# Block-diagonal gate products of an RG-LRU with hi and lo parts stacked along the contraction

## The chip, the cores and the metric

The kernel runs on one core of a Trainium2 chip. The metric is the device time of one execution in microseconds; several runs are made and their median counts.

## The reference, cut to what matters

Two layers (DEPTH = 2) act on x of 256 tokens by 1024 features, all in float32. A layer is a feed-forward half step, a mixing block with two branches, a second feed-forward half step and a gate on a per-layer input. The change lies in the first branch of the mixing block, a gated linear recurrence over time (RG-LRU):

```python
def rg_lru(x, w_a, b_a, w_x, b_x, lam):          # 16 blocks of 64 x 64
    xb = x.reshape(B, S, RNN_BLOCKS, RNN_BW)
    r = jax.nn.sigmoid(jnp.einsum('bsnc,ncd->bsnd', xb, w_a).reshape(B, S, C) + b_a)
    i = jax.nn.sigmoid(jnp.einsum('bsnc,ncd->bsnd', xb, w_x).reshape(B, S, C) + b_x)
    log_a = -RG_C * r * jax.nn.softplus(-lam)
    a = jnp.exp(log_a)
    mult = jnp.sqrt(-jnp.expm1(2.0 * log_a))
    u = mult * (i * x)
    # h[t] = a[t] * h[t-1] + u[t]

for i in range(DEPTH):
    x = x + 0.5 * swiglu_ffn(...)
    rx, rgate, q, k, v, f_logit, ga, gb = split(rms_norm(x) @ w_in[i])
    ya = (rg_lru(causal_dwconv(rx)) * gelu(rgate)) @ w_rnn_out[i]
    yb = forgetting_attention(q, k, v, f_logit) @ w_attn_out[i]
    x = x + (sigmoid(ga) * ya + sigmoid(gb) * yb) @ w_o[i]
    x = x + 0.5 * swiglu_ffn(...)
    x = x + sigmoid(rms_norm(x) @ w_pg + b_pg) * (p[i] @ w_pe)
```

## The kernel before

Features lie on the 128 partitions, in KT = 8 tiles `m` of 128, and the S = 256 tokens lie along a row. Every product keeps float32 accuracy by splitting each operand into a part `hi`, rounded to the matmul type float32r, and the rest `lo`; TensorE (PE) then adds three products, hi by hi, hi by lo and lo by hi (`mm3`, L297 to L300, and `mm3m`, L302 to L305), or a variant with one 512-column and one 256-column matmul (`mm2`, L338 to L341), whose two halves `total` (L375 on ACT, L376 on DVE) adds.

Weights come from memory in 1 MB loads on SyncE's queue. Each load is cut into units of 128x1024. For each unit ScalarE (ACT) writes the hi part `wh` (L96) and VectorE (DVE) subtracts to get the lo part `wl` (L97). There are five buffers for `wh` and five for `wl`, so a new unit can be split only when PE is done with the unit five before.

The code states an order, with small steps that are put off (`defer`) and called one or two at a time between units (`tick`). The framework then orders the instructions of each engine anew, by a model of its own of how long each takes. Each engine runs its list strictly in that order: an instruction that waits holds up all that stand behind it.

In the mixing block `mix` of each layer the work runs like this:

- For each tile m the recurrence's input is projected, convolved on DVE into `xc` (L512) and split into `xch` (ACT, L516) and `xcl` (DVE, L517).
- The values v (four weight units) are computed. Between them and in the first q group, `gates(m)` (from L542) makes the two gate products of tile m. The weights of two 64x64 blocks stand in a 128x128 matrix whose other two quarters are zero. Three matmuls of 256 columns make the first gate, r, and three more the second, i. ACT applies a tanh to each (`thr` L548, `thi` L549). The step `s1` bounds thr (DVE, L553) and forms the decay `a` and its companions on ACT; `s2` forms `tq` and multiplies i into `xc` on DVE.
- When all eight tiles are there, `root` takes one square root over all of `tq` on ACT (L564, with a load of its function table ahead of it). `scan(m)` multiplies (L569) and runs the recurrence (L570) on DVE.
- Products for q and k (`qk`), their squared sums (ACT `qsq` L647, DVE L649) and their norms, whose power runs on GpSimd (POOL, L652), are followed by attention for eight heads. `step_a` transposes (`tr`, L685) and splits q and k (`aq` L692 and `ak` L693 are their lo parts). `step_b` makes the scores `s` (L704) and the probabilities `pr`. `step_c` transposes those (`pt`, L729) and ACT copies them to `ph` (L731). `step_d` makes the head's output `o<-ph,vh` (L739).
- Between these steps PE is given "filler" products `f` (L298 to L300) for the gates of the branches. Then follow `ya` (W_rnn_out), `yb` (W_attn_out) and, on four PSUM banks in turn, the output product `o<-mg` (L338 to L341).

Two pools matter. Tiles of 128x512 (`work2`, tag `w2`) have three buffers. PSUM has four banks called mm and four called at.

## Time and profile before

| | |
|---|---|
| median of 3 runs | 1318.01 us (1317.98 to 1318.56) |
| the profiled execution, whole | 1318.03 us |
| its span from first to last instruction | 1316.3 us (1.7 us lie around it) |
| PE busy | 1306.8 us, 99% of the span |
| DVE busy | 1069.5 us, 81% |
| ACT busy | 813.5 us, 62% |
| POOL busy | 34.8 us, 3% |
| granted PE clock | full in every slice |

The profile is one execution of the kernel. A row of a timeline gives the start in us, the duration in us, the engine, the source line and operation, the tiles written and read, and in brackets the idle time ahead of it with the instruction that ended it. Matmuls overlap: each lasts longer than the distance to the next one, so what one costs is the distance between starts.

### The profile page before, as it was taken

Reading aid. Unit: us, or ns where it says so; the run is one execution under the profiler, and the core shown is the slowest. Engines: PE = TensorE matmul, PEld = TensorE weight load, DVE = VectorE, ACT = ScalarE, POOL = GpSimd, SP = SyncE. Lnnn points to the kernel's source line nnn. Section 1 sums busy time; section 2 is a strip of 40 time slices with the busy share of each in tenths; the row PEclk is TensorE's granted clock in tenths of the full one; section 3 lists DMA queues with packets and bytes.
Section 4 is the critical chain, followed back from the end, with each engine's and each line's share of the span. In section 5 each row is a group of like instructions: output and inputs, shape, how many; then the busy total and the mean of one; then the engine's idle time right before and its main releaser. Section 6 shows DMA issues by size and latency. Waiting matters only on the chain.

```text
span 1316.3 us, 21929 instructions
## 1 busy us (share of the span) xinstructions
PE 1306.8 (99%) x8376; PEld 1188.0 (90%) x8376; DVE 1069.5 (81%) x2100; ACT 813.5 (62%) x1479; POOL 34.8 (3%) x44
## 2 busy tenths in 40 slices
PE   9999999999999999999999999999999999999997
PEld 8888899889999888889988888998899898888896
DVE  7998769899676899876789887697996678998765
ACT  6665657867664666565556556578676555665653
POOL 1000000020000000000000000000200000000000
PEclk9999999999999999999999999999999999999999
DMA  8654664445444555456545546654443445554660
GB/s 294 240 184 155 218 226 165 178 167 176 158 161 161 197 188 192 163 180 234 177 177 192 192 134 228 220 188 160 171 180 138 161 170 206 186 183 154 220 226 32
DMA packets 37256, 241.22 MB, mean 183 GB/s; under 512 B 4128, under 2 KB 4256, under 8 KB 14368
## 3 DMA queue, kind: packets, MB, share of 16 engines
q1 hardware_dynamic: 36864, 239.30, 51.6%
q8 instruction: 66, 1.08, 0.3%
q10 hardware_dynamic: 288, 0.52, 0.1%
q14 instruction: 38, 0.31, 0.1%
HBM read 238.76 MB, written 1.05 MB: 182 GB/s over the span
## 4 chain that ended last, share of the span: by engine, by line
PE 99%; DMA 0%; ACT 0%; DVE 0%; POOLq 0%; DVEq 0%; issue 0%
PE mm L341 20%; PE mm L339 11%; PE at L341 11%; PE at L339 6%; PE f L298 3%; PE f L300 3%; PE f L299 3%; PE qk L303 2%; PE qk L305 2%; PE qk L304 2%; PE mm L300 2%; PE mm L298 2%; PE mm L299 2%; PE mm L338 2%; PE ya L341 2%; PE at L338 2%
## 5 line engine op out<-in xcount | busy, mean ns | idle before, releaser
L97 DVE TENSOR_TENSOR wl<-wr,wh 128x1024 fp32r<-128x1024 f32 (+2 forms) x476 | 538.3, 1133 | 143.6 <-ACT wh L96 137.6
L96 ACT ACTIVATE wh<-wr 128x1024 fp32r<-128x1024 f32 (+2 forms) x476 | 467.3, 986 | 298.8 <-PE mm L341 91.3
L341 PE MATMUL mm<-h,wh 128*128 128x512 f32 x616 | 219.1, 394 | 0.0
L341 PE MATMUL at<-h,wh 128*128 128x512 f32 x616 | 218.6, 394 | 0.0
L339 PE MATMUL mm<-h,wl 128*128 128x256 f32 x704 | 182.3, 280 | 0.0
L339 PE MATMUL at<-h,wl 128*128 128x256 f32 x704 | 181.7, 281 | 0.0
L341 PE MATMUL mm<-f,wh 128*128 128x512 f32 x504 | 176.9, 394 | 0.0
L339 PE MATMUL mm<-f,wl 128*128 128x256 f32 x528 | 144.1, 280 | 0.0
L339 PEld LDWEIGHTS at<-h,wl 128*128 128x128 f32 x704 | 132.0, 188 | 8.8 <-ACT h L331 0.7
L339 PEld LDWEIGHTS mm<-h,wl 128*128 128x128 f32 x704 | 131.8, 188 | 7.8 <-DVE wl L97 0.4
L341 PEld LDWEIGHTS mm<-h,wh 128*128 128x128 f32 x616 | 115.6, 188 | 22.6
L341 PEld LDWEIGHTS at<-h,wh 128*128 128x128 f32 x616 | 114.9, 188 | 21.9
L341 PEld LDWEIGHTS mm<-f,wh 128*128 128x128 f32 x504 | 94.4, 188 | 20.8
L300 PE MATMUL f<-h,wl 128*128 128x256 f32 x384 | 108.5, 283 | 0.0
L298 PE MATMUL f<-h,wh 128*128 128x256 f32 x384 | 108.5, 283 | 0.0
L299 PE MATMUL f<-h,wh 128*128 128x256 f32 x384 | 108.1, 282 | 0.0
L339 PEld LDWEIGHTS mm<-f,wl 128*128 128x128 f32 x528 | 99.4, 188 | 2.1
L299 PEld LDWEIGHTS f<-h,wh 128*128 128x128 f32 x384 | 72.4, 188 | 0.1
L298 PEld LDWEIGHTS f<-h,wh 128*128 128x128 f32 x384 | 72.3, 188 | 0.1
L300 PEld LDWEIGHTS f<-h,wl 128*128 128x128 f32 x384 | 72.4, 188 | 0.0
L375 ACT ACTIVATE sum<-mm 128x256 f32<-128x256 f32 x112 | 40.1, 375 | 50.6 <-PE mm L341 50.4
L376 DVE TENSOR_TENSOR sum<-mm,sum 128x256 f32<-128x256 f32 x112 | 45.0, 419 | 14.8 <-ACT sum L375 14.8
(297 smaller groups left out, 2746.9 us busy)
## 6 DMA issues: line engine op xcount, KB each, us to landing
wr<-in_w2i SPq DMA_DIRECT2D x44, 1024.0 KB, 4.8
wr<-in_w1i SPq DMA_DIRECT2D x41, 1024.0 KB, 4.8
wr<-in_wf SPq DMA_DIRECT2D x32, 1024.0 KB, 4.8
wr<-in_w1o SPq DMA_DIRECT2D x32, 704.0 KB, 4.0
wr<-in_w2o SPq DMA_DIRECT2D x32, 704.0 KB, 4.1
wr<-in_wqk SPq DMA_DIRECT2D x16, 1024.0 KB, 4.8
wr<-in_wv SPq DMA_DIRECT2D x8, 1032.0 KB, 4.8
wr<-in_wro SPq DMA_DIRECT2D x8, 1024.0 KB, 4.8
```

Of the source, the lines that this page charges most:

```text
L96: self.nc.scalar.activation(out=hi[:, c], in_=src[:, c], func=AF.Copy)
L97: self.nc.vector.tensor_tensor(out=lo[:, c], in0=src[:, c], in1=hi[:, c].bitcast(F32), op=ALU.subtract)
L298: T.matmul(ps, lhsT=wh, rhs=xh, start=first, stop=False)
L299: T.matmul(ps, lhsT=wh, rhs=xl, start=False, stop=False)
L300: T.matmul(ps, lhsT=wl, rhs=xh, start=False, stop=last)
L303: T.matmul(ps, lhsT=xh, rhs=wh, start=first, stop=False)
L304: T.matmul(ps, lhsT=xh, rhs=wl, start=False, stop=False)
L338: T.matmul(ps, lhsT=wh, rhs=t, start=True, stop=False, skip_group_check=True)
L339: T.matmul(ps[:, 0:S], lhsT=wl, rhs=t[:, 0:S], start=False, stop=False, skip_group_check=True)
L341: T.matmul(ps, lhsT=wh, rhs=t, start=False, stop=last, skip_group_check=True)
L375: A.activation(out=o, in_=ps[:, S:], func=AF.Copy)
L376: V.tensor_tensor(out=o, in0=ps[:, 0:S], in1=o, op=ALU.add)
```

## The change

In `mix`, tiles are now handled in pairs. After the split of an odd tile m, three transfers on GpSimd's queue rearrange `xch` and `xcl` of tiles m-1 and m: the upper 64 rows of `xch` go to a scratch tile `sw`, the lower 64 rows of `xcl` go to the upper rows of `xch`, and `sw` goes to the lower rows of `xcl`. From then on `xch` holds hi and lo of the lower block, and `xcl` those of the upper block. Each transfer moves 64x512 numbers, 128 KB, and there are 12 of them in a layer.

The weights are laid out to match: each 64x64 block stands twice, once against hi and once against lo. Both gates of a block fill the 128 columns, the two in swapped order for the upper block. Two matmuls (hi and lo part of the weights) now make both gates of one block, four per tile in place of six. Of each block's 128 output rows, 64 belong to r and 64 to i. The tanh of each half goes to a 128x512 tile `tg`; two transfers of 64x256 numbers (64 KB) per tile, on GpSimd's queue, bring the i rows to their place in `thi`, and the bounding of thr is done in two operations of 64 partitions each. In a layer that makes 16 such transfers, so 28 transfers in all and 56 in two layers.

Last, the multiply of `scan` is marked to stay in program order.

```diff
@@ split of the recurrence's input
                 A.activation(out=xch[:, m], in_=xc[:, m], func=AF.Copy)
                 V.tensor_tensor(out=xcl[:, m], in0=xc[:, m], in1=xch[:, m].bitcast(F32), op=ALU.subtract)
+                if m % 2:
+                    c = slice(m - 1, m + 1)
+                    t = work2(F32R, "sw")[lower].rearrange("p (m s) -> p m s", m=2)
+                    G.dma_start(out=t, in_=xch[upper, c])
+                    G.dma_start(out=xch[upper, c], in_=xcl[lower, c])
+                    G.dma_start(out=xcl[lower, c], in_=t)
             defer(conv, split)
@@ gates(m)
-            for g in range(2):
-                c = slice((m * 2 + g) * P, (m * 2 + g + 1) * P)
-                mm3(ps[:, g * S:(g + 1) * S], wg_hi[:, c], wg_lo[:, c], xch[:, m], xcl[:, m], True, True)
+            for b, xs in enumerate((xch, xcl)):
+                c = slice((m * 2 + b) * P, (m * 2 + b + 1) * P)
+                T.matmul(ps[:, b * S:(b + 1) * S], lhsT=wg_hi[:, c], rhs=xs[:, m], start=True, stop=False)
+                T.matmul(ps[:, b * S:(b + 1) * S], lhsT=wg_lo[:, c], rhs=xs[:, m], start=False, stop=True)
             thr, thi, th, a2 = work(s="thr"), work(s="thi"), work(s="th"), work(s="a2")
-            A.activation(out=thr, in_=ps[:, 0:S], func=AF.Tanh, scale=0.5, bias=hcol(l, "ba", m))
-            A.activation(out=thi, in_=ps[:, S:], func=AF.Tanh, scale=0.5, bias=hcol(l, "bx", m))
+            t2 = work2(s="tg")
+            for b, own, other in ((0, lower, upper), (1, upper, lower)):
+                c = slice(b * S, (b + 1) * S)
+                A.activation(out=t2[:, c], in_=ps[:, c], func=AF.Tanh, scale=0.5, bias=hcol(l, ("ba", "bx")[b], m))
+                G.dma_start(out=thi[own], in_=t2[other, c])
             def s1():
-                V.tensor_scalar(out=thr, in0=thr, scalar1=-1.0, scalar2=None, op0=ALU.max)
+                for b, own in ((0, lower), (1, upper)):
+                    V.tensor_scalar(out=thr[own], in0=t2[own, b * S:(b + 1) * S], scalar1=-1.0, scalar2=None,
+                                    op0=ALU.max)
@@ scan(m)
-            V.tensor_tensor(out=tq[:, m], in0=tq[:, m], in1=xc[:, m], op=ALU.mult)
+            tc.keep_in_program_order(V.tensor_tensor(out=tq[:, m], in0=tq[:, m], in1=xc[:, m], op=ALU.mult))
```

The framework's order changes with it, on every engine. Lines 564, 569, 704, 729 and 739 of the kernel before are lines 580, 585, 720, 745 and 755 of the changed one.

On ACT, around the square root of layer 0, the kernel before had this order (a number behind a name tells tiles of one name apart; `wh_3097` and `wh_3117` of before are the same two units as `wh_3129` and `wh_3149` of the changed kernel):

```order
L96 ACTIVATE wh_3031<-wr_3029 128x1024
L622 ACTIVATE dh_3021<-dc_3016 128x256
L555 ACTIVATE th_2886<-thr_2884,sp 128x256
L556 ACTIVATE a_2887<-a_2506 128x256
L96 ACTIVATE wh_3053<-wr_3029 128x1024
L564 ACT_TABLE_LOAD
L564 ACTIVATE tq_2507<-tq_2507,tiny 128x2048
L647 ACTIVATE qsq_3069<-qk_2976 128x512
L96 ACTIVATE wh_3097<-wr_3095 128x1024
L96 ACTIVATE wh_3117<-wr_3095 128x1024
```

The changed kernel has this one:

```order
L96 ACTIVATE wh_3129<-wr_3127 128x1024
L570 ACTIVATE a_2518<-thr_2953,sp 128x256
L571 ACTIVATE th_2955<-thr_2953,sp 128x256
L663 ACTIVATE qsq_3110<-qk_3007 128x512
L572 ACTIVATE a_2956<-a_2518 128x256
L96 ACTIVATE wh_3149<-wr_3127 128x1024
L580 ACT_TABLE_LOAD
L580 ACTIVATE tq_2519<-tq_2519,tiny 128x2048
L96 ACTIVATE wh_3171<-wr_3169 128x1024
```

The table load and the square root have moved two weight units later. On PE, between the last transpose `tr` of the first head and that head's first score product, there stood 37 matmuls (8 `qk` of 512 columns and 29 `f` of 256); now 24 `f` stand there. Counted from the program's start, that score product has 21 matmuls of 256 columns less ahead of it: 16 of the gates and 5 `f`. On DVE, between the square root and the lo part `ak` of that head, there now stand 6 multiplies, 6 scans, 4 reduces, 4 products `qk`, 8 operations of four columns, 7 units `wl` and the lo part `aq`.

On PE, at the last head's probabilities, where the `ya` products end and the `yb` products begin, the changed kernel of layer 0 has:

```order
L339 MATMUL ya_4738<-yr_3674,wl_4636 128x256
L341 MATMUL ya_4738<-yr_3674,wh_4635 128x512
L745 MATMUL pt_4308<-ident,pr_4261 128x128 x3
L755 MATMUL o_4348<-ph_4312,vh_2520 128x256
L338 MATMUL yb_4763<-ot_3375,wh_4662 128x512
```

The head's output now stands right behind its transposes. Before, 26 matmuls of `ya` stood between the last of them and the output product. On ACT, ahead of the copy to `ph` that this product reads, the changed kernel has the total of the last `ya` bank and one weight unit:

```order
L738 ACTIVATE pr_4261<-pr_4261,rs_4263 128x128
L738 ACTIVATE pr_4261<-pr_4261,rs_4263 128x256
L375 ACTIVATE sum_4759<-ya_4738 128x256
L96 ACTIVATE wh_4766<-wr_4764 128x1024
L747 ACTIVATE ph_4312<-pt_4308 128x384
```

These stood in the same order in the kernel before, so what moved is PE's work between the transposes and their user.

On PE in the output product, between the last matmul of the first bank, `o_5036`, and the first of the fifth, `o_5159`, which takes over that bank, the changed kernel has 11 matmuls (7 of 512 columns, 4 of 256):

```order
L341 MATMUL o_5036<-mg_4928,wh_4897 128x512
L341 MATMUL o_5037<-mg_4928,wh_4932 128x512
L341 MATMUL o_5097<-mg_4928,wh_4968 128x512
L339 MATMUL o_5097<-mg_4928,wl_4969 128x256
L341 MATMUL o_5097<-mg_4928,wh_4968 128x512
L341 MATMUL o_5129<-mg_4928,wh_5002 128x512
L339 MATMUL o_5129<-mg_4928,wl_5003 128x256
```

Before, 21 stood there, among them all of the fourth bank, which the changed kernel begins ahead of the first bank's last matmul. ACT's and DVE's order is the same as before there: a weight unit, then the totals of the first two banks.

On GpSimd, layer 0 has this queue, whose transfers are sent in order:

```order
L524 DMA sw_2358<-xch_2195 64x512
L525 DMA xch_2195<-xcl_2196 64x512
L524 DMA sw_2436<-xch_2195 64x512
L526 DMA xcl_2196<-sw_2358 64x512
L525 DMA xch_2195<-xcl_2196 64x512
L524 DMA sw_2514<-xch_2195 64x512
L526 DMA xcl_2196<-sw_2436 64x512
L525 DMA xch_2195<-xcl_2196 64x512
L526 DMA xcl_2196<-sw_2514 64x512
L524 DMA sw_2581<-xch_2195 64x512
L563 DMA thi_2613<-tg_2616 64x256 x2
```

Before, GpSimd had no transfers, and in this stretch nothing but the eight powers of the q and k norms, which now stand behind the last `thi` transfer.

## Rows read from the trace of the kernel before

**Rows 1.** The page, busy time: engine, us busy (share of span), instructions.

```profile
PE 1306.8 (99%) x8376; PEld 1188.0 (90%) x8376; DVE 1069.5 (81%) x2100; ACT 813.5 (62%) x1479; POOL 34.8 (3%) x44
```

**Rows 2.** All waits of PE: line, releaser, us in total, times, longest.

```profile
PE warm L865 <- POOL ones L193: 1.1, 1, 1.1
PE at L338 <- ACT wh L96: 0.3, 1, 0.3
```

**Rows 3.** Window of layer 0: busy us of PE, PEld, DVE, ACT, POOL; PE clock.

```profile
200.00:302.00 102.00, 102.00 (x633) 93.41 (x632) 91.59 (x195) 73.80 (x125) 11.25 (x8) 1.00 0.50 179
```

**Rows 4.** Timeline of PE: first and twelfth matmul of the first gate pair.

```profile
222.76 0.28 PE L298 MATMUL g<-xch,wbh 128*128 128x256 f32 x1
...
224.06 0.28 PE L300 MATMUL g<-xch,wbl 128*128 128x256 f32 x1
```

**Rows 5.** Timeline of ACT around the square root of layer 0.

```profile
263.72 1.06 ACT L96 ACTIVATE wh<-wr 128x1024 fp32r<-128x1024 f32 x1 [0.32 <-PE qk L305]
264.80 1.28 ACT L564 ACT_TABLE_LOAD   x1
266.09 2.01 ACT L564 ACTIVATE tq<-tq,tiny 128x2048 f32<-128x2048 f32 x1
...
274.90 1.06 ACT L96 ACTIVATE wh<-wr 128x1024 fp32r<-128x1024 f32 x1 [1.75 <-PE qk L305]
```

**Rows 6.** Timeline of DVE from the square root to the first head's q and k.

```profile
268.13 2.44 DVE L569 TENSOR_TENSOR tq<-tq,xc 128x256 f32<-128x256 f32 x7 [2.09 <-ACT tq L564]
...
271.08 3.01 DVE L570 TENSOR_TENSOR_SCAN xc<-a,tq 128x256 f32<-128x256 f32 x5
...
287.39 0.22 DVE L650 TENSOR_SCALAR s<-s,s 128x4 f32<-128x4 f32 x1
287.52 0.69 DVE L655 TENSOR_TENSOR qk<-qk,s 128x512 f32<-128x512 f32 x1
288.13 1.22 DVE L97 TENSOR_TENSOR wl<-wr,wh 128x1024 fp32r<-128x1024 f32 x1
...
291.46 0.47 DVE L693 SCALAR_TENSOR_TENSOR ak<-tr,gqk,ak 128x256 fp32r<-128x256 f32 x1
```

**Rows 7.** Timeline of PE: last transpose of the first head, and its first score.

```profile
287.02 0.27 PE L685 MATMUL tr<-ident,qk 128*128 128x128 f32 x1
...
292.42 0.70 PE L704 MATMUL s<-ak,aq 128*128 128x256 f32 x5
```

**Rows 8.** Timeline of PE: the last head's transposes and the product that uses them.

```profile
390.60 0.38 PE L729 MATMUL pt<-ident,pr 128*128 128x128 f32 x2
...
395.35 0.28 PE L739 MATMUL o<-ph,vh 128*128 128x256 f32 x1
```

**Rows 9.** Timeline of ACT at the same place.

```profile
390.33 0.38 ACT L375 ACTIVATE sum<-ya 128x256 f32<-128x256 f32 x1 [1.46 <-PE ya L341]
390.61 1.05 ACT L96 ACTIVATE wh<-wr 128x1024 fp32r<-128x1024 f32 x1
391.56 0.48 ACT L731 ACTIVATE ph<-pt 128x384 fp32r<-128x384 f32 x1
```

**Rows 10.** Timelines of ACT and DVE when the first output banks are done.

```profile
427.08 1.06 ACT L96 ACTIVATE wh<-wr 128x1024 fp32r<-128x1024 f32 x1 [4.50 <-PE o L341]
...
429.31 0.75 DVE L376 TENSOR_TENSOR sum<-o,sum 128x256 f32<-128x256 f32 x2
```

**Rows 11.** The page, DMA issues: KB each, median us from issue to landing.

```profile
out_dram<-xo ACTq DMA_DIRECT2D x2, 256.0 KB, 2.1
p<-in_pT SPq DMA_DIRECT2D x2, 256.0 KB, 5.1
```

**Rows 12.** Groups of POOL's instructions: us busy, mean ns, idle ahead, releaser.

```profile
L652 POOL TENSOR_TENSOR s<-s,mhalf 128x4 f32<-128x4 f32 x16 | 22.5, 1406 | 173.9 <-DVE s L650 172.5 <-DVE s L653 1.5
```

**Rows 13.** Timeline of ACT: hi copies of the second and the last tile.

```profile
213.50 0.42 ACT L516 ACTIVATE xch<-xc 128x256 fp32r<-128x256 f32 x1
...
239.45 0.40 ACT L516 ACTIVATE xch<-xc 128x256 fp32r<-128x256 f32 x1
```

More of the change, by code (lines that the diff above doesn't have):

```diff
@@ L502, in mix @@
         xcl = big([P, KT, S], F32R, "xcl")
+        lower, upper = slice(0, 64), slice(64, P)
         def rx_post(m, ps):
@@ L1026, in _layout @@
     wv = wv.transpose(0, 1, 3, 2, 4).reshape(L, 4, P, 6 * VC)
-    wg = np.zeros((L, P, KT, 2, P), np.float32)
+    wg = np.zeros((L, 2, 64, KT, 2, 2, 64), np.float32)
     for i, t in enumerate((g["rg_wa"], g["rg_wx"])):
@@ L1030, in _layout @@
         for b in range(2):
-            wg[:, b * 64:(b + 1) * 64, :, i, b * 64:(b + 1) * 64] = t[:, :, b].transpose(0, 2, 1, 3)
+            wg[:, :, :, :, b, i ^ b] = t[:, :, b].transpose(0, 2, 1, 3)[:, None]
     wg = wg.reshape(L, P, KT * 2 * P)
@@ L1052, in _layout @@
     put("mbb", g["merge_b"][:, D:])
-    put("ba", g["rg_ba"])
-    put("bx", g["rg_bx"])
+    rb, ib = (g[n].reshape(L, KT, 2, 64) for n in ("rg_ba", "rg_bx"))
+    put("ba", np.concatenate([rb[:, :, 0], ib[:, :, 0]], axis=2))
+    put("bx", np.concatenate([ib[:, :, 1], rb[:, :, 1]], axis=2))
     put("pb", g["ple_b_gate"])
```

## The prediction, made before the changed kernel ran

> **What bounds the kernel now.** I read the busy times first. PE works for 1306.8 of the 1316.3 us of the span [rows 1]. Next come PE's waits: there are two, both at the start, 1.4 us together [rows 2]. In the stretch with the gates, the root and the first scores of layer 0, PE is busy for 102.00 of 102.00 us at full clock, and DVE, at 91.59 us, has a tenth of the stretch to spare [rows 3]. So the time is the sum of PE's matmuls, and two things can move it: fewer matmuls, or a wait of PE that was not there. PE runs its list in order, so a wait is paid in full and nothing behind it can slip ahead. The question for each edit is therefore whether the other engines still have each operand ready when PE comes to it.
>
> **The matmuls removed.** The first gate pair starts a matmul at 222.76 and its twelfth at 224.06, so one costs 1.30 / 11 = 0.118 us [rows 4]. The change takes two of six away in each of 8 tiles and 2 layers: 32 x 0.118 = -3.8 us, or 1.9 us in a layer. They lie on the path whole, as PE has no idle time there. The lengths of the other matmuls stay.
>
> **What is added on ACT, DVE and GpSimd.** The tanh operations are as many and as long as before. DVE gets 16 bounding operations more, 8 in a layer; each costs between 0.13 us, the distance of a four-column operation, and 0.61 us, that of one of 128x512 [rows 6]. I take 0.2, as they have 256 columns and half the partitions: 1.6 us in a layer, at most 5, against the 10 us that DVE has free in that stretch [rows 3], and none of it on PE's path. If that cover were gone it would be added to the first place below. GpSimd's 56 transfers cost PE nothing if they land in time. For that I ask how long one may take. The hi copy of the second tile ends at 213.92 [rows 13], and two chained transfers must be through before the first gate matmul at 222.76 [rows 4]: (222.76 - 213.92) / 2 = 4.4 us each. No transfer between two tiles of the chip's memory stands in the trace. The nearest rows have 256 KB: 2.1 us for stores on an otherwise quiet end, 5.1 us for a load in the midst of the weights' [rows 11]. I take a value of some 3 us, since 128 KB is half of either, and keep both ends: at 2.1 the transfers are covered, at 5.1 they are late by 2 x 5.1 - 8.8 = 1.4 us. The price of sending one from GpSimd is not in the trace either; that engine's only work here, the powers, takes 1.4 us each [rows 12], which I take as the upper end. They can bring no gain of their own, as nothing is removed for them.
>
> **The three places where the order opens a wait.** The framework has ordered all engines anew, and at three places in each layer PE reaches a user earlier than its operand.
>
> *First scores.* The square root moves two weight units later on ACT. Units there come at a distance of (274.90 - 263.72) / 4 = 2.8 us [rows 5], so the unit ahead of the root starts at 263.72 + 5.6 = 269.3, less the 1.9 us that PE saves before, 267.4. Behind it come the unit itself (1.08 us to the table load), the table load (1.29) and the root with the start of DVE (268.13 - 266.09 = 2.04) [rows 5, 6]: DVE starts its multiplies at 271.8. What now stands on DVE up to `ak`, at the distances of rows 6: 7 units `wl` of 1.14, 6 multiplies of 0.335 (2.36 us for seven), 6 scans of 0.60 (3.01 for five), 4 products `qk` of 0.61 and 4 reduces of about the same, 8 small operations of 0.13, `aq` 0.33 and `ak` 0.47. That is 8.0 + 2.0 + 3.6 + 2.4 + 2.4 + 1.0 + 0.8 = 20.2 us, so `ak` is ready at 292.0. PE gets to the score earlier than before: 292.42 [rows 7], less 1.9 for the gates, less 5 x 0.118 for the fillers behind it now, 289.9. PE waits 2.1 us. Before, `ak` ended at 291.93 [rows 6], half a microsecond ahead of the score, so this place had little cover to give away. Behind the waiting score stand only fillers, which could have run but can't pass. The bounds: 0.7 us if ACT catches up half a unit, 1.4 us, of the delay in its idle time (it stands idle for 1.75 us ahead of one unit, [rows 5]), and 3.2 if DVE loses the time of one late `wl`, 1.1.
>
> *Last head.* The output product stands right behind its transposes. In the kernel before they start at 390.60 and it follows at 395.35, with 26 matmuls between [rows 8], and those hid ACT's copy. ACT does three things after the last `ya` matmul: the total (0.28), a weight unit (0.95) and the copy to `ph` (0.48), 390.33 to 392.04 or 1.71 us [rows 9]. The last matmul ends 0.16 us after the next can start (0.39 long in its rows, 0.23 apart), and three transposes take about 0.32, so PE waits 1.71 + 0.16 - 0.32 = 1.55 us. That ACT stands idle for 1.46 us ahead of the total [rows 9] says that it will be ready for it and not late as well. If the unit's buffer were not yet free, this would be longer by up to 1.0; if the framework's two engines shift so that the unit comes ahead of the total, it would be 0.95 shorter.
>
> *Output product.* The fifth bank takes the place of the first, whose total must have been read. From the end of the first bank's last matmul ACT does a weight unit and the total, DVE a unit and its own total: from 427.08 to about 0.4 after 429.31, 2.63 us [rows 10]. PE has 11 matmuls in between, 7 x 0.233 + 4 x 0.118 = 2.10, and starts them 0.16 before that end. The wait is 2.63 + 0.16 - 2.10 = 0.7 us. It could be nothing, if DVE's unit comes later than the total, or 1.2, if DVE's unit is not done when the total is.
>
> Each place stands in layer 1 with the same rows between, so I count it twice: 2 x (2.1 + 1.55 + 0.7) = 8.7. The sum, against the profiled execution of 1318.03 us (the median is 1318.01, so nothing is to be shifted; the 1.7 us outside the span stay): 1318.0 - 3.8 + 8.7 = **1322.9 us**. With the low ends of the three, 2 x (0.7 + 0.6 + 0) - 3.8 = -1.2, so 1316.8; with the high ends, 2 x (3.2 + 2.5 + 1.2) - 3.8 = +10.0, so 1328.0. Keeping the scan's multiply in program order is part of the first place: the DVE row of multiplies and scans alternates now where seven multiplies stood together [rows 6], which costs no work.
>
> **Rivals.** *The transfers are late.* What speaks for it: 5.1 us for that load, and three transfers of a pair depend on each other. GpSimd's queue is in order, so a transfer that waits for a tile holds up those of the next. At 5.1 us the first gates wait 1.4 us. The last tile's hi copy comes at 239.45 [rows 13], and its gates, the `thi` transfers and the root behind them slip again, by as much each; three slips of 1.3 to 1.4 us are 4 us in a layer, 8 in both: about 1331. If sending one takes 2 us or more, the 28 transfers in a layer take 56 us of the 75 or so between the first copy and the first scores, and I would expect up to 1345. Against it: at half the bytes the transfer should be under 4.4 us.
>
> The Trainium skill, SBUF — State Buffer, section "SBUF: two separate sides", says that a transfer issued by GpSimd can stand still while VectorE runs certain operations that take the port both share, and gives 620 ns alone against 3100 ns beside a copy. No run here shows it yet. By it each transfer would be some 2.5 us longer, which turns my 3 us into this rival's 5.1 or more. Its page DMA: Bandwidth & Descriptors, section "Anatomy of one DMA — SWDGE (gpsimd) path", gives 2.0 us and the bytes at 436 GB/s, an estimate of 2.3 us for 128 KB, by which the sum would stay as it is.
>
> *The waits do not appear.* If the other engines run ahead by 2 us at all three places, only the removed matmuls are left: 1318.0 - 3.8 = 1314.2. For it speaks ACT's idle time ahead of its units [rows 5, 9]; against it, that PE's user is too close in order at the last head whatever runs ahead, since the chain begins with a matmul just before.
>
> *Only that wait appears.* If the first scores and the output product are covered, -3.8 + 2 x 1.55 = -0.7: 1317.3, no change that can be told. If one of the two is half there, it is 1319.
>
> **How the numbers follow.** A difference under 0.2%, 2.6 us, can't be told from no change here: the bounds are 1315.4 and 1320.6. I give the forecast with its three waits 55%, the late transfers 24%, only some waits 15%, none 6%. So faster 0.07, no change 0.15, slower 0.78. The likeliest case is 1322.9. The range leaves out the case of no wait and the thinnest part of the last rival below (about 1 in 10), and the very slow end of late transfers above (as much): 1317 to 1334.
>
> **What would show it right or wrong.** In the changed kernel's profile PE's waits must name three lines twice: the score product released by DVE's `ak` with about 2 us, the output of a head released by ACT's `ph` with about 1.5, and the fifth bank of the output product released by DVE's total with about 0.7. PE's busy time must fall by 3.8 us. The gate matmuls must show no wait for a transfer, and 128 KB must land within 4.4 us of its issue. A wait at the gates, or a `tq` multiply that waits for a `thi` transfer, speaks for late transfers. If the waits are other ones, the way I read the order is wrong and not only a size.

## The result and the profile after

The changed kernel takes **1329.22 us** (median of 6 runs, 1327.94 to 1332.60), the one before 1318.03 beside it (6 runs, 1317.98 to 1318.56). The ratio is 1.0087, with an interval of 1.0075 to 1.0099: slower, as forecast, and inside the range, but by 11.2 us where the sum said 4.9. The profiled execution took 1329.16 us, with a span of 1327.4.

Busy time and the waits of PE (line, releaser, us in total, times, longest), to be set against [rows 1, 2]:

```profile
PE 1306.9 (98%) x8344; PEld 1185.9 (89%) x8344; DVE 1075.1 (81%) x2116; ACT 813.4 (61%) x1479; POOL 64.2 (5%) x100
```

```profile
PE s L720 <- DVE ak L709: 3.8, 2, 1.9
PE o L755 <- ACT ph L747: 2.9, 2, 1.5
PE f L298 <- DVE qk L671: 1.6, 1, 1.6
PE o L338 <- DVE sum L376: 1.4, 2, 0.7
PE warm L881 <- POOL ones L193: 1.1, 1, 1.1
PE f L298 <- ACT qsq L663: 0.6, 1, 0.6
```

The three places of the forecast are there, twice each. A fourth stands beside the first: a filler `f`, once released by `qk` and once by `qsq`. There are 32 matmuls fewer, yet PE's busy time did not fall by 3.8 us, as it was to do: rows of PE that run at half clock, or start behind a wait, are longer. In the kernel of all places below, which has neither behind its start, it is 1302.2 us.

The timeline of PE (start, duration, engine, line, tiles, and in brackets the wait and its releaser) at the first scores of layer 0, against [rows 7]:

```profile
286.92 0.27 PE L701 MATMUL tr<-ident,qk 128*128 128x128 f32 x1
287.82 0.36 PE L298 MATMUL f<-h,wh 128*128 128x256 f32 x1 [0.64 <-ACT qsq L663]
...
290.62 0.28 PE L300 MATMUL f<-h,wl 128*128 128x256 f32 x1
292.81 0.77 PE L720 MATMUL s<-ak,aq 128*128 128x256 f32 x5 [1.91 <-DVE ak L709]
...
293.65 0.29 PE L298 MATMUL f<-h,wh 128*128 128x256 f32 x1
...
294.17 0.41 PE L298 MATMUL f<-h,wh 128*128 128x256 f32 x1
294.38 0.41 PE L299 MATMUL f<-h,wh 128*128 128x256 f32 x1
...
297.30 0.28 PE L298 MATMUL f<-h,wh 128*128 128x256 f32 x1
```

And one window in the last stretch (busy us of PE, PEld, DVE, ACT, POOL; granted PE clock):

```profile
294.00:295.00 1.00, 1.00 (x6) 1.00 (x6) 1.00 (x3) 0.42 (x1) 0.00 (x0) 0.50 0.69 279
```

Two readings. PE waits 0.64 and 1.91 us. Then, from about 293.9 to 297.2, the fillers start 0.21 us apart where 0.118 is usual, and the granted clock is 0.50, the lower of the two levels (1.2 GHz). From 293.65 to 297.30 there are 18 distances, 3.65 us in place of 18 x 0.118 = 2.12: **1.5 us** that no list of waits shows.

I price a wait by the distance between starts, less the usual one. The bracket counts from the end of the matmul ahead, which reaches 0.16 us past the point where the next one usually starts (0.28 long, 0.118 apart), so it shows 1.91 us at the scores where PE lost 2.07. In layer 0 that is 0.88 at the filler, 2.07 at the scores, 1.63 at the last head and 0.88 at the output product; in layer 1 it is 1.86, 2.08, 1.63 and 0.86. Together 11.9 us. With the matmuls, the half clock and 0.6 us at the very end of the span (below): -3.8 + 11.9 + 1.5 + 0.6 = 10.2 of the 11.1 us by which the profiled execution is longer. Of the rest, some 0.7 us lie in layer 1, in distances too small to be laid to one row.

The six runs fit this: the two shortest (1327.94 and 1328.06) have mean granted clocks of 0.999 and 0.998, the two longest (1330.61 and 1332.60) 0.995. How often the clock falls seems to differ from run to run, though only one of them has a trace; the six runs before the change all lie within 0.6 us.

### The profile page after: what moved, and what is told of

The parts are those of the page before. It is cut to its first block, busy times and chain, and to the rows that moved or that the text cites. A ratio compares the mean times of both kernels' runs of the same rounds, so it can differ in the third digit from the quotient of the medians.

```text
span 1327.4 us, 22034 instructions
## 1 busy us (share of the span) xinstructions
PE 1306.9 (98%) x8344; PEld 1185.9 (89%) x8344; DVE 1075.1 (81%) x2116; ACT 813.4 (61%) x1479; POOL 64.2 (5%) x100
## 4 chain that ended last, share of the span: by engine, by line
PE 89%; DVE 4%; ACT 3%; issue 2%; DMA 2%; POOL 0%; POOLq 0%; DVEq 0%; ACTq 0%
PE mm L341 20%; PE mm L339 11%; PE at L341 11%; PE at L339 6%; PE f L300 3%; PE f L298 3%; PE f L299 3%; PE mm L298 2%; PE mm L300 2%; PE mm L299 2%; PE mm L338 2%; PE ya L341 2%; PE at L338 2%; DVE wl L97 1%; PE o L341 1%
## 5 line engine op out<-in xcount | busy, mean ns | idle before, releaser
L428 POOL TENSOR_TENSOR R<-s,mhalf 128x2 f32<-128x2 f32 x8 | 8.2, 1027 | 1089.6 <-DVE s L425 1089.6
```

Source lines behind the costliest of these rows:

```text
L428: G.tensor_tensor(out=R, in0=ms, in1=mhalf[:, 0:TT], op=ALU.pow)
```

## The experiments

The theory after the result: the whole loss is waits at places where the new order puts a user too close to its operand, plus the half clock behind them. The rivals: the transfers themselves cost the time, or the marker on the scan does, or the late root is the one cause of the first place.

### Which half of the change

**The marker alone.** In the kernel before, the multiply of `scan` is kept in program order:

```diff
-            V.tensor_tensor(out=tq[:, m], in0=tq[:, m], in1=xc[:, m], op=ALU.mult)
+            tc.keep_in_program_order(V.tensor_tensor(out=tq[:, m], in0=tq[:, m], in1=xc[:, m], op=ALU.mult))
```

> The kernel before with only the marker on the scan's multiply; no transfer, six products per tile. If the marker by itself spoils the order at the first scores (it spreads the scans between the weight units), PE must wait there and the time rises by 2 to 6 us, to 1320 to 1324. If it takes the stacked products as well, as I think, PE shows no wait beyond the two at the start and the time stays at 1318.0 within 0.5 us.

Measured: 1317.98 us, ratio 0.9999 (0.9989 to 1.0008). No wait of PE outside the start.

**The products alone.** The changed kernel with that marker taken off again.

> The changed kernel without the marker: seven multiplies and seven scans stand in a row again on DVE. If the marker caused the wait of the first scores, that wait (3.0 and 3.9 us in the two layers) goes and the time falls to about 1322. If the late root causes it, the wait only moves: the long run of multiplies and scans now stands ahead of weight units, PE waits for wl at a qk product instead, some 2 to 4 us in a layer, and the time stays between 1326 and 1332. The waits of the last head (1.5) and of the output product (0.7) stay in both cases.

Measured: 1328.61 us, ratio 1.0081 (1.0064 to 1.0098). The waits of PE:

```profile
PE qk L303 <- DVE qk L671: 3.2, 2, 1.6
PE o L755 <- ACT ph L747: 2.9, 2, 1.5
PE qk L304 <- DVE wl L97: 2.7, 2, 1.4
PE o L338 <- DVE sum L376: 1.4, 2, 0.7
```

So the loss comes with the products and not with the marker. Without the marker the first scores don't wait; `qk` rows do, by 5.9 us in place of 6.0 (brackets, fillers included). The last two places are the same to a tenth.

**The transfers alone.** The kernel before, with 56 transfers of the same sizes at the same points of the code, into tiles that nobody reads.

```diff
+                if m % 2:
+                    c = slice(m - 1, m + 1)
+                    t = work2(F32R, "sw").rearrange("p (m s) -> p m s", m=2)
+                    G.dma_start(out=t[0:64], in_=xch[64:P, c])
+                    G.dma_start(out=t[64:P], in_=xcl[0:64, c])
+                    G.dma_start(out=t[64:P], in_=t[0:64])
...
+            t2 = work2(s="tg")
+            G.dma_start(out=t2[0:64, 0:S], in_=thi[64:P])
+            G.dma_start(out=t2[64:P, S:], in_=thi[0:64])
```

> The kernel before with the 56 transfers of the change, same sizes, same queue, same points in the program, but into scratch that nobody reads; six products per tile as before. If the transfers cost something by themselves (they slow the weights' loads, DVE or ACT, or hold GpSimd's powers back), the time rises, by 4 to 8 us if that is where the part of the loss lies that my sum had not got. If only what waits for them matters, PE shows no new wait and the time stays at 1318.0 within 1 us.

Measured: 1319.87 us, ratio 1.0013 (1.0004 to 1.0022): 1.8 us longer than the runs of before beside it, and more than the 1 us allowed for. PE has no wait but those at the start, so by themselves the transfers make a small part of the 11.2 us, though they are not free. The profiled execution, 1319.20 us, is one of the shortest and 1.2 us longer than that of before. Of these, 0.6 lie among the matmuls and 0.6 behind the last one: from the start of the last matmul to the end of the span it is 9.1 us, where it was 8.5. In all six kernels with 56 transfers this stretch is 9.1 us, in the eight with fewer 8.2 to 8.6.

### What the transfers do to the rest

**No transfers of the gates.** ACT writes the tanh of each half straight to the rows where it belongs, in four operations of 64 rows; `tg` and 32 transfers are gone.

```diff
-                A.activation(out=t2[:, c], in_=ps[:, c], func=AF.Tanh, scale=0.5, bias=hcol(l, ("ba", "bx")[b], m))
-                G.dma_start(out=thi[own], in_=t2[other, c])
+                bias = hcol(l, ("ba", "bx")[b], m)
+                A.activation(out=thr[own], in_=ps[own, c], func=AF.Tanh, scale=0.5, bias=bias[own])
+                A.activation(out=thi[own], in_=ps[other, c], func=AF.Tanh, scale=0.5, bias=bias[other])
...
-                for b, own in ((0, lower), (1, upper)):
-                    V.tensor_scalar(out=thr[own], in0=t2[own, b * S:(b + 1) * S], scalar1=-1.0, scalar2=None,
-                                    op0=ALU.max)
+                V.tensor_scalar(out=thr, in0=thr, scalar1=-1.0, scalar2=None, op0=ALU.max)
```

> The changed kernel without the 32 gate transfers: ACT writes each tanh straight to its place, in four operations of 64 partitions a tile in place of two of 128, and the bounding is one operation again. The three transfers of a pair stay. If late gate transfers are what makes the root late, the group of waits at the first scores (3.0 and 3.9 us, start to start) shrinks to under 1 us in a layer, and with it the time to 1323 or less. If the order and DVE's load do it, a wait of some 3 us in a layer stays between the last qk product and the first score, whatever line it shows at, and in both layers alike; the last head and the output product have a new order here and show no wait, so the time is then 1318.0 - 3.8 + 2 x 3.3 + 0.6 at the end = 1321.4, plus up to 2 if the clock falls.

Measured: 1323.32 us, ratio 1.0044 (1.0029 to 1.0059). One wait is left, and the granted clock falls behind it in each layer:

```profile
PE f L298 <- DVE qk L669: 5.1, 2, 2.6
```

```profile
290.39 0.39 PE L298 MATMUL f<-h,wh 128*128 128x256 f32 x1 [2.58 <-DVE qk L669]
```

```profile
293.00:294.00 1.00, 1.00 (x7) 1.00 (x7) 1.00 (x5) 0.00 (x0) 0.26 (x1) 0.50 0.60 246
```

By distances of starts the wait costs 2.74 and 2.71 us, alike in the two layers, and the half clock 1.7 in each: -3.8 + 5.45 + 3.4 = +5.1, and 5.2 was measured. So without the gate transfers the wait of some 3 us in a layer stays. A new order has closed the last head and the output product, and the extra 1 us of layer 1 is gone. That the transfers gave this 1 us is not shown, since the order changed with them.

**No transfers of hi and lo.** ACT and DVE write the stacked tiles directly, in 64-row pieces; the gate transfers stay.

```diff
+                A.activation(out=xch[lower, m], in_=xc[lower, m], func=AF.Copy)
+                A.activation(out=sw[upper], in_=xc[upper, m], func=AF.Copy)
+                A.activation(out=xcl[lower, m], in_=xc[upper, m], func=AF.Copy)
+                V.tensor_tensor(out=xch[upper, m], in0=xc[lower, m], in1=xch[lower, m].bitcast(F32), op=ALU.subtract)
+                V.tensor_tensor(out=xcl[upper, m], in0=xc[upper, m], in1=sw[upper].bitcast(F32), op=ALU.subtract)
```

> The changed kernel without the 24 stacking transfers: ACT and DVE write hi and lo of each block half straight to their rows (three copies on ACT and two subtractions on DVE per tile in place of one each). The gate transfers stay. If the stacking transfers are part of the loss at the first scores, less than 1 us of wait in a layer stays there. If the order does it, PE's waits come at other places, as in every new order: by the order of this one some 1 us at the fillers and 3 us at the last head in each layer, so 1318.0 - 3.8 + 2 x 4.3 + 0.6 = 1323.4, up to 1327.

Measured: 1327.12 us, ratio 1.0067 (1.0050 to 1.0083), a tenth above the 1327 that was named as the upper end; the 1323.4 had no half clock in it. The loss has moved once more, mainly to the last head's transposes, and the clock falls behind those in both layers:

```profile
PE pt L743 <- ACT pr L736: 3.7, 2, 1.8
PE f L298 <- DVE qk L669: 1.8, 4, 0.7
PE o L753 <- ACT ph L745: 1.2, 2, 0.6
```

### Moving the places

**Two places moved.** In the changed kernel the last head's output is called inside the first pair of `yb` products, and the fourth output bank (m = 3) begins only behind the three before it, as in program order.

```diff
-                slots[4 + (5 * h + 1) // 2 + i].append((f, h))
+                if (f, h) != (step_d, NH - 1):
+                    slots[4 + (5 * h + 1) // 2 + i].append((f, h))
...
+        yb = [atbank("yb") for _ in range(MB)]
+        pair(yb[0], yb[1], ot, lambda: step_d(NH - 1))
...
+                    pin[0] = m in (3,)
```

> The changed kernel with PE's order mended at two places: the last head's output product stands behind seven tiles of the first two yb products, and the fourth bank of the output product starts only when the first is done. No work is left out. If these two waits are made by the order alone, both go, at 1.6 + 0.9 us from start to start in each layer: 1329.2 - 5.0 = 1324.2, and the wait at the first scores stays as it is. If something behind them is late by itself (ACT or DVE behind with their work), the waits turn up at the next user and the time stays near 1329.

Measured: 1323.11 us, ratio 1.0038 (1.0025 to 1.0051): 6.1 us less than the changed kernel. Those two places cost 2 x 1.63 + 0.88 + 0.86 = 5.0 there, which gave the forecast of 1324.2, and both have left the list; the further 1.1 us are not followed to their rows.

```profile
PE s L724 <- DVE ak L713: 3.9, 2, 1.9
PE f L298 <- ACT wh L96: 1.6, 1, 1.6
PE f L298 <- DVE qk L675: 0.8, 1, 0.8
```

**Four places.** No gate transfers, the two places moved, the last head's transposes also among the `yb` products, and the second half of the q and k products (`cb` = 1) given banks of both kinds, which changes the order around the first scores.

```diff
-            banks = [two[t * (1 - cb)]("qk") for t in range(TT)]
+            banks = [two[t]("qk") for t in range(TT)]
...
+        yb = [atbank("yb") for _ in range(MB)]
+        w0, w1 = W.next(), W.next()
+        tiles(yb[0], w0, ot, range(KT - 1))
+        step_c(NH - 1)
+        tiles(yb[1], w1, ot, range(KT - 1))
+        step_d(NH - 1)
```

> The products of the change, the stacking transfers kept, the gate transfers replaced by ACT as in the fourth experiment, and the order mended where PE waited: the second q and k groups use a bank of either kind, so that the fillers find a free one, the last head's two steps stand inside the yb products, and the fourth output bank starts behind the first. If the loss is made by the order alone, nearly all waits go: 1318.0 - 3.8 + 2 x 1.5 + 0.6 = 1317.8, as fast as the kernel before or a little faster (1316.5 to 1319). If the transfers cost something of their own beside the end, or DVE's load makes a wait at any order, the time stays above 1321.

Measured: **1316.77 us**, ratio 0.9990 (0.9981 to 1.0000). A little is left: two of the three transposes had slipped behind `yb` rows, and the output product waits again.

```profile
PE o L759 <- ACT ph L751: 1.2, 2, 0.6
...
PE g L559 <- DMA xch<-xcl: 0.5, 1, 0.5
```

**The same with both kinds of banks for the first unit's second half only** (`two[t * (1 - cb * w)]`).

> The same as the seventh with one difference: of the second q and k groups only the first uses banks of either kind. The last head's wait should go as well, at the price of some tenths at the fillers: 1317 to 1320 if the order alone counts, above 1321 if not.

Measured: 1317.68 us, ratio 0.9997 (0.9987 to 1.0006). A filler waits for `qk` on DVE, 1.0 us in each layer.

**All places.** As the four places, and the first `yb` rows of the second unit are kept behind all three transposes:

```diff
+        pin[0] = True
         tiles(yb[1], w1, ot, range(KT - 1))
+        pin[0] = False
```

> Kernel: that of e7_four_places, with one thing more: the first yb[1] tile of the last head's unit stands behind all three transposes of the probabilities, where in e7 two of the three had slipped behind yb tiles and the exponential's result came 1.2 us late for the output product in each layer. Theory (the whole loss of the change is waits at places of TensorE's order, and each goes where its place is moved): the two waits at the output product go, no other comes: 1316.8 - 2 x 1.2 = 1314.4 us, up to 1315 with the wait of 0.5 to 0.7 at a gate transfer that stays in layer 1; that is the matmuls' 3.8 us off the time of before, whole. Rival (the drained pipeline is only pushed to another row: the softmax of the last head has a chain that must end somewhere): the wait comes back at a transpose or at a scores row with 1 us or more per layer, and the time stays at 1316.5 to 1318.

Measured: **1314.19 us** (6 runs, 1314.10 to 1314.66), ratio 0.9970 (0.9958 to 0.9982): faster than the kernel before. PE's busy time is 1302.2 us, PE waits only at the start, and the clock stays full until the last matmul.

```profile
PE warm L897 <- POOL ones L193: 1.1, 1, 1.1
PE at L340 <- ACT wh L96: 0.6, 1, 0.6
PE at L343 <- DVE wl L97: 0.3, 1, 0.3
```

ACT's root, DVE's lo part of the first head's keys, and PE's first score in this kernel:

```profile
275.50 2.01 ACT L582 ACTIVATE tq<-tq,tiny 128x2048 f32<-128x2048 f32 x1
```

```profile
286.02 0.47 DVE L711 SCALAR_TENSOR_TENSOR ak<-tr,gqk,ak 128x256 fp32r<-128x256 f32 x1
```

```profile
287.92 0.70 PE L722 MATMUL s<-ak,aq 128*128 128x256 f32 x5
```

The root starts 5 us later than in the changed kernel (270.54), and nothing waits: `ak` ends at 286.49, 1.4 us ahead of the score.

**The places alone.** The kernel before with the same moves, without the new products and without transfers.

> Kernel: the one before the change, with nothing but the moved places of e9_all_places (two bank kinds for the second half of the q and k products, the last head between the yb tiles, the two orders kept); the gate products keep their six matmuls per tile and there are no transfers. Theory (the places give nothing where no wait was; e9 is faster only by the matmuls): within 0.5 us of before, 1317.6 to 1318.6. Rival (the places are an improvement of their own, and the stacked products are worth less than 3.8 us): 1314 to 1317. If the new order opens a wait here, it shows as a row among TensorE's waits, and the time is above 1318.6 by it.

Measured: 1318.04 us, ratio 1.0000 (0.9991 to 1.0009). The moves give nothing by themselves. So the 4.0 us by which the kernel of all places is faster than the runs of before beside it (its interval is 2.4 to 5.5) are the 32 matmuls. The traces agree: from the first matmul's start to the last one's it is 1302.9 us, where it was 1306.8.

**The places, with the gate transfers back.**

> Kernel: that of e9_all_places, but with the tanh results brought to their rows by the 32 transfers of the change again, so all 56 transfers run. Theory (the transfers cost TensorE almost nothing of themselves; what they do is to change the times by which the order was made): the first scores and the output product stay without a wait, and the end of the span grows by the 0.6 us that the dummy transfers cost: 1314.2 + 0.6 = 1314.8 if nothing else moves. But the order is another one here: ahead of the last head's transposes the last five matmuls of the head before it now stand between yb rows, two yb matmuls behind their reader's source, so the copies on ScalarE behind them can open waits of up to 2 us at yb or at the head's output in each layer, 1319 to 1322. Rival (the gate transfers are late for TensorE or ScalarE, or steal time from VectorE): waits at the gates, at the first scores or at filler rows come back with 1.5 us or more a layer, and the time is 1318 or more by these rows.

Measured: 1322.45 us, ratio 1.0035 (1.0021 to 1.0050). The first score and the output product stay covered; the last heads wait, as their order changed again:

```profile
PE o L761 <- ACT ph L753: 3.3, 2, 1.7
PE s L724 <- DVE ak L713: 1.3, 2, 0.7
...
PE yb L343 <- ACT ot L328: 0.9, 2, 0.5
```

No wait of PE names a transfer, and the gates, the first scores and the fillers show none, so the rival's rows are not there on PE; over the whole run ACT waits 4.0 us and DVE 2.3 us for transfers. The theory's 1314.8 is not reached either: the waits are those that the new order was said to open, and the time is half a microsecond above the 1319 to 1322 named for them. By starts the waits come to 3.4 us in each layer, and the end of the span is 0.9 us longer (9.1 against 8.2): 7.7 of the 8.3 us over the kernel of all places. The other 0.6 are not laid to a row; the transfers alone had as much among the matmuls. The waits of layer 0 lie at 392 to 401 us, and its last transfer lands at 264.69, so it is the order that came with the transfers, and not their time, that makes most of the cost. But all places is without the 32 gate transfers, and no run with all 56 is faster than the kernel before.

### The root on ACT

**Root early.** In the changed kernel, ACT's work for the weight units from the second behind the filler on is ordered behind the root.

```diff
-            A.activation(out=tq, in_=tq, func=AF.Sqrt, scale=1.0 / 16.0, bias=tiny)
+            r = A.activation(out=tq, in_=tq, func=AF.Sqrt, scale=1.0 / 16.0, bias=tiny)
+            for i in W.acts[W.pos + 2:]:
+                tc.add_manual_dep(i.ins, r.ins.name, mybir.DependencyInfo(mybir.DependencyClass.NoSync,
+                                  mybir.DependencyReason.DATA), reason="root first")
```

> Kernel: after, with one more order on ScalarE: the work of the weight units from the second behind the filler on stands behind the square root of the norms, so that the root starts as early on ScalarE as it did before the change; all else, the transfers too, as in after. Theory A (the first scores wait because the root, and with it the chain of 20 us on VectorE, starts late): the wait at the first scores and the one at the filler shrink from 2.95 and 3.94 us to under 1 in each layer, and the time falls by 4 to 6 us to 1323 to 1325. Theory B (VectorE's own load up to the scaled keys is what ends late, or the rows on which the root lets go are now late themselves): an earlier root only moves the wait, to a transpose or a projection row ahead of it (some 0.8 us) and to the filler (some 2.5 us), and the time stays within 1326 to 1329. Moving ScalarE's work may also let the weight units' own results come late: then TensorE waits at gate or u rows on ScalarE, and the time is 1329 or more.

Measured: 1324.97 us (4 runs, 1323.85 to 1327.57), ratio 1.0053 (1.0040 to 1.0067). The profile is of the longest run, with three half-clock stretches' worth of time, 10.2 us at the lower level. Its waits:

```profile
PE tr L706 <- DVE qk L676: 3.6, 3, 1.4
PE f L300 <- DVE rs L741: 2.7, 2, 2.2
...
PE qk L306 <- DVE wl L99: 0.5, 1, 0.5
```

The root starts at 268.50, only 2.0 us earlier, since it then waits for the last `tq` of DVE. The wait at the first scores is gone, and 4.2 us in layer 0 (1.17 + 0.67 + 2.38 by starts) stand at a transpose, a `qk` and a filler, more than the 2.95 that they replace; in layer 1 it is 3.6 in place of 3.9. Theory A got the time and was wrong on the mechanism; theory B got the waits. The time fell because the last head and the output product, in another order, wait no more.

## Why the prediction came out as it did

**The bound and the sign: right.** PE had no slack, so each removed matmul counted whole and each wait too. The removed matmuls are worth -3.8 us; the kernel of all places is 4.0 us faster than the kernel before, and its moves without the products change nothing.

**First scores: the right place, too small a term.** It was to cost 2 x 2.1 = 4.2 us and cost 2.95 + 3.94 = 6.9, filler and score together, since both end at the same `ak`. The rows of ACT and DVE, against [rows 5, 6]:

```profile
270.54 2.01 ACT L580 ACTIVATE tq<-tq,tiny 128x2048 f32<-128x2048 f32 x1
```

```profile
272.58 0.42 DVE L585 TENSOR_TENSOR tq<-tq,xc 128x256 f32<-128x256 f32 x1 [0.84 <-ACT tq L580]
...
292.19 0.47 DVE L709 SCALAR_TENSOR_TENSOR ak<-tr,gqk,ak 128x256 fp32r<-128x256 f32 x1
```

From the first multiply to the end of `ak` DVE took 292.66 - 272.58 = 20.1 us, forecast 20.2, and PE would have reached the score at 289.9, as forecast. The term that was mis-sized in layer 0 is the root's place in time: DVE began at 272.58, not at 271.8. Another 0.15 us pass from the end of `ak` to the start of the score. In layer 1 PE came to the place 1.0 us earlier as seen from the root (last transpose to root 15.40 us in place of 16.38). "Each place stands in layer 1 with the same rows between, so I count it twice" was the weak step: equal rows are not equal times. The bound of 3.2 for one layer was too low for layer 1.

The late root is also too narrow a cause. Against the kernel before, `ak` ends only 0.7 us later (292.66 against 291.93), while PE would come 2.6 us earlier (289.86 against 292.42): its early arrival makes most of the wait. The kernel of the places with the gate transfers back shows this apart. Its root (270.67) and its `ak` are as late as in the changed kernel, but behind the last transpose 50 `f` stand ahead of the score in place of 24, and the score does not wait:

```profile
292.06 0.48 DVE L713 SCALAR_TENSOR_TENSOR ak<-tr,gqk,ak 128x256 fp32r<-128x256 f32 x1
```

```profile
293.99 0.70 PE L724 MATMUL s<-ak,aq 128*128 128x256 f32 x5
```

So a later root alone opens no wait, and an earlier one only moved the waits (root early). What counts is when PE comes to the score and when DVE is done with `ak`; in the kernel of all places `ak` is done sooner, since only 5 multiplies, 4 scans and 3 units `wl` stand on DVE between the root and `ak`.

**The filler ahead of it** was not in the forecast at all. It waits for a PSUM bank, and I had followed only operands there, although for the output product I had asked for the bank as well. It adds little of its own in layer 0, since the score waits for `ak` anyway.

**Last head: right.** 1.55 us was forecast and 1.63 came, from ACT's three steps in the order that was read from the order lists (rows of ACT, then PE):

```profile
398.55 0.38 ACT L375 ACTIVATE sum<-ya 128x256 f32<-128x256 f32 x1 [0.64 <-PE ya L341]
398.83 1.05 ACT L96 ACTIVATE wh<-wr 128x1024 fp32r<-128x1024 f32 x1
399.78 0.48 ACT L747 ACTIVATE ph<-pt 128x384 fp32r<-128x384 f32 x1
```

```profile
400.31 0.39 PE L755 MATMUL o<-ph,vh 128*128 128x256 f32 x1 [1.47 <-ACT ph L747]
```

From 398.55 to 400.26 it is 1.71 us, the forecast figure to the hundredth.

**Output product: right** in place and chain, 0.7 forecast, 0.88 and 0.86 by starts; the small difference is not followed to its rows.

**Transfers: the value of 3 us was too low, and the cover was just enough.** Transfers on GpSimd's queue (KB each, median us from issue to landing):

```profile
thi<-tg POOLq DMA_DIRECT2D x32, 64.0 KB, 4.7
sw<-xch POOLq DMA_DIRECT2D x8, 128.0 KB, 2.5
xch<-xcl POOLq DMA_DIRECT2D x8, 128.0 KB, 4.5
xcl<-sw POOLq DMA_DIRECT2D x8, 128.0 KB, 4.4
```

```profile
217.15 0.52 POOL L525 DMA_DIRECT2D xch<-xcl  x1 [2.26 <-DVE xcl L520]
```

That 128 KB would land within 4.4 us of the issue is not borne out: two of the medians lie at 4.4 and 4.5, and single transfers take up to 6.3. Two chained ones take 2.5 + 4.5 = 7.0 us by the medians, of the 8.8 there were. The first pair's took more, since the second was sent only at 217.15, when DVE's `xcl` was there. By the trace it landed at 222.15, 0.6 us ahead of the first gate matmul (222.72). So no gate matmul waits here, but with little to spare: in the kernel of four places one does, for 0.5 us. To send one takes 0.5 us, a third of the upper end I took. The rival of late transfers came near in time (1331) and not by its mechanism: PE never waits for one in the changed kernel, and in each layer its waits at and behind the first scores come after the last landing (264.65 and 921.85). ACT and DVE do wait, at the tanh and at `xc`, the multiply that reads `thi` (their waits over the whole run):

```profile
ACT tg L562 <- DMA xcl<-sw: 2.5, 4, 1.4
ACT tg L562 <- DMA thi<-tg: 2.4, 2, 1.5
```

```profile
DVE xc L576 <- DMA thi<-tg: 4.4, 3, 1.8
```

That these waits are a part of the late root is not shown. Gate transfers are not needed for one: without them the root starts later still, at 276.39 (no transfers of the gates) and 275.50 (all places).

The Trainium skill, SBUF — State Buffer, section "SBUF: two separate sides", gives 620 ns for a transfer alone and 3100 ns beside a copy on VectorE. An estimate from these two, 2.5 us more for a transfer that is held up, would take the 2.5 us of `sw` to 5.0, near the 4.4 to 4.7 of the others; but all of them stand in the same stretch of the same queue, and no row shows what held one up, so the rows don't decide it. The Trainium skill, DMA: Bandwidth & Descriptors, section "Anatomy of one DMA — SWDGE (gpsimd) path", gives 2.0 us and the bytes at 436 GB/s, an estimate of 2.2 us for 64 KB and 2.3 us for 128 KB. `sw` comes near that; the others take twice as long, and 64 KB longer than 128 KB, so here the measured times count.

**What was not in the sum:** the half clock, 1.5 us in this run, and 0.6 us at the end of the span. The first came behind a wait, so a sum of waits alone is too low. The sum said 4.9 us and the profiled execution is 11.1 longer. Of the 6.2 us between them the first scores with their filler make 2.7, the other two places 0.5, the half clock 1.5 and the end 0.6; 0.9 are not laid to a row.

**The chances.** "The waits do not appear" gave 1314.2; the kernel of all places reached 1314.19, so the number was right for an order in which each place is covered, though that kernel does without the 32 gate transfers. The 6% were for the order as it was given, and there the waits did appear. That 1329.22 lies in the range is in part luck: the high ends of the three places gave 1328.0, and the room above it was left for late transfers.

## What to carry to other kernels

When one engine is full, a saving on it can be undone several times over by a new order (3.8 us saved, 11.2 us lost in all), so read each user and its operand, and its bank, in the new order, in every repetition of it. Take the waits away at their places (another bank, work between producer and user, an order kept) before judging the edit, and run the moved places alone as a control. Price a wait by the distance between starts, and allow for the half-clock stretch that can follow it.

## What the runs showed of the hardware

- PE's granted clock can fall to 0.50 behind a wait of about 2 us (after 1.91 us in the changed kernel, after 2.58 us with no gate transfers), and then stays there for 3.4 us, which costs 1.5 to 1.7 us. It is not certain: a wait of 1.92 us in layer 1 of the changed kernel left the clock full.
- A kernel with 56 transfers on GpSimd's queue ends some 0.6 us later behind its last matmul (9.1 us in six kernels); with 24, 32 or none it does not (8.2 to 8.6 in eight). Why is not shown.
- ACT can read 64 rows and write them to the other 64 partitions as fast as to their own: 471 ns against 467 in the kernel of all places. Four operations of 64 rows took the place of two of 128 rows and 470 ns, so it cost 17 us of ACT's time (830.4 against 813.4) to do without the 32 gate transfers, and PE waits for none of it.
